# Two mixer layers and a mixture of experts: products in PSUM, an early weight split, solid first loads, stores ahead of a branch

## The chip, the cores and the metric

One core of one Trainium2 chip runs the kernel. The time is the device time of one execution in microseconds. The core has TensorE (PE, and PEld for its weight loads), VectorE (DVE), ScalarE (ACT), GpSimd (POOL) and SyncE (SP, which issues the loads here). SBUF is the working memory, PSUM holds TensorE's results in eight banks of 2 KB a partition.

## The reference

256 tokens of width 1024 go through two layers. Each layer projects the tokens, runs a gated causal convolution (31 taps on 512 channels) and a retention of 4 heads with rotary embedding, gates the retention, projects back and normalises. Layer 0 then has a dense SwiGLU, layer 1 a mixture of eight SwiGLU experts, two a token:

```python
for l in range(DEPTH):
    mix = hybrid_mixer(x, w_in[l], w_out[l], conv_w[l], conv_b[l], ...)
    x = layer_norm(ALPHA * x + mix, ln1_g[l], ln1_b[l])
    f = swiglu(x, ...) if l % 2 == 0 else moe_swiglu(x, router, moe_w1, moe_w3, moe_w2)
    x = layer_norm(ALPHA * x + f, ln2_g[l], ln2_b[l])
# in the mixer:   qh = rotary(q);  kh = rotary(k);  r = silu(g) * group_norm(retention(qh, kh, v))
# in the experts: gate = softmax(top-2 logits);  y = sum of gate * (silu(xe @ w1[e]) * (xe @ w3[e])) @ w2[e]
```

## The kernel before, in words

**Operands.** Every large product is three matmuls of rounded parts (`mm3`, L152): each float is split into a high part and a remainder. `parts` (L107) does it: ACT casts the high part, then DVE, or POOL where a unit says so, subtracts. All weights come as units of 1 MB ([128, 2048] floats), and each half of a unit is split by itself. So for every half that TensorE uses there is an ACT cast (L109) and a subtraction (L110).

**The order of weights.** It is written out by hand. `plan` appends halves to a stream, `W.take()` hands out the next one, and `W.ahead(n)` makes sure that n halves beyond the used ones are loaded and split; `emit` issues the load of a unit on SP when its first half is split. Every engine works through its instructions in program order. So where `W.ahead` stands decides where the casts and subtractions stand in ACT's, DVE's and POOL's queues. SP only waits for a buffer to come free and runs far ahead. Load buffers go round in a ring (`seq`, `pools`); behind the mixers the ring gets further places (`raw2`), in memory that the mixers leave.

**Start (L228 to L238).** The transposed tokens (`xf`) and the first two weight units arrive in quarters of 256 KB, alternating on SP. Each is split as it comes. 40 filler matmuls run ahead of the first product.

**Mixer (L367 to L640, once per layer).** The 124 multiply-adds of the convolution are DVE instructions (L391, one operand and the result in PSUM) that `fill` puts between the other steps in counted portions; the last taps of one channel group run on TensorE (`taps`, L403). `rotary` (L437) makes q and k of one token tile: a product into the scratch tile t2 in SBUF (L441), a product into qk (L444), and their sum (L446). The gate: TensorE projects g (`proj`), `taps` follows, then ACT writes silu(g) into the SBUF tile `sgt` (L584) and DVE multiplies `rz` by it (L585), per token tile, with a portion of `fill` behind each. TensorE transposes `rz` (`turn_r`, L497) and starts the output product (`wout_r`, L506). Meanwhile DVE ends the convolution, whose last sum is L394; its result is transposed (L516), normalised and joins the output product.

**Router (end of the mixer in layer 1).** The last normalisation (`ln_end`, L272 and L278) is done per token tile; the first tile's is followed by its transposes, logits (L320) and split for the gather, on POOL (L627). Then `W.ahead(2)` puts the split of the first expert unit there, `choose` (L303) picks the two experts on DVE, and the second tile does the same; `W.ahead(4)` splits the second unit. Filler matmuls, a prefix sum (L724 to L728), `rk` (L731), a permutation matrix P (L742) and gather matmuls (L751) follow.

**Experts.** 56 blocks of eight halves of w1 and w3 and four of w2. It ends with the sum of the last expert (`add`, L774; for tile 1 ACT and POOL), statistics, and `moments` (L971). Then comes a branch (L982) around a large body that is run only when an expert gets more than 128 tokens, which it does not here. Behind the branch stand the last normalisation (L1019, L1026) and the four stores: two on SP, two on ACT's queue.

Of the kernel before, what the change touches and what calls it, by code (L numbers as in the profile page):

```python
# [37 lines left out]
POOL_END = ((1, 0),)  # L38
ACT_END = (1,)
# [13 lines left out]
class Unit:  # L53
    def __init__(self, src, eng=None, n=1, at=None):
        self.src, self.eng, self.n, self.at, self.raw = src, eng, n, at, None
# [19 lines left out]
def tile_hybrid(ctx: ExitStack, tc, xT_in, x_in, ws, wm, cols, lnp, gnp, router, ident_in, rot, mask_in, out):  # L75
# [51 lines left out]
    def fetch(unit):  # L127
        if unit.raw is None:
            unit.raw = new_raw()
            n = 2048 // unit.n  # L130
            for q in range(unit.n):
                nc.sync.dma_start(unit.raw[:, n * q:n * q + n], unit.src[:, n * q:n * q + n])
        return unit.raw
# [88 lines left out]

    def part_w(i, q, r):
        o = W.made[2 * i + q // 2]
        parts(o[0][:, half(q % 2)], o[1][:, half(q % 2)], r[:, half(q)])

    for q in range(4):
        k = slice(2 * q, 2 * q + 2)  # L228
        nc.sync.dma_start(xf[:, k, :], xT_in[:, k, :])
        nc.sync.dma_start(r0[:, half(q)], ws[0][:, half(q)])  # L230
        parts(xh[:, k, :], xl[:, k, :], xf[:, k, :])
        part_w(0, q, r0)
    for q in range(4):
        nc.sync.dma_start(r1[:, half(q)], ws[1][:, half(q)])
# [132 lines left out]
    def mixer(l, psum, mp, me, heads, then):  # L367
# [209 lines left out]
        sgt = mp.tile([128, NT, 512], F32, tag="qkT", name="sgt")  # L577
# [16 lines left out]
        Wc += [W.take(0) for _ in range(4)]  # L594
        wout_r(0, 0)
# [30 lines left out]
        if l > 0:  # L626
            parts(xn[0][:, 0, :], xn[1][:, 0, :], x[:, 0, :], gp)  # L627
            W.ahead(2)
            choose(0, pl[:, 0, :])
        turn_x(NT - 1, psum)  # L630
# [3 lines left out]
        else:  # L634
# [3 lines left out]
            W.ahead(4)  # L638
# [94 lines left out]
    def gather(rk_of, n, pls, pt):  # L733
# [6 lines left out]
        for t in range(NT):  # L740
            for i in range(n):
                v.tensor_scalar(P[:, t, 128 * i:128 * i + 128], iota, rk_of(i, t), None, op0=ALU.is_equal)  # L742
# [3 lines left out]
        for k in range(0, KD, 2):  # L746
# [8 lines left out]
            for i in range(n):  # L755
                parts(gs[i][0][:, k:k + 2, :], gs[i][1][:, k:k + 2, :], p[:, :, i, :])
# [8 lines left out]
    def put(ys, PT, t):  # L765

        p = ptp.tile([128, 512], F32, tag="tp", name="pc")
# [4 lines left out]
    def add(p, t, h, g):  # L772
        o = acc[:, t, half(h)]
        v.scalar_tensor_tensor(o, p, g, o, op0=ALU.mult, op1=ALU.add)  # L774
# [74 lines left out]
    g0 = tokens_of(0)  # L849
    cnt = mo.tile([128, 1], F32, name="cnt")  # L850
# [105 lines left out]
    ps = [[put(ys[h], PT, t) for t in range(NT)] for h in range(2)]  # L956
    for h in range(2):
        for t in range(NT):
            o = acc[:, t, half(h)]
            if t in ACT_END:  # L960
                part = raw2[3 + h].tile([128, 512], F32, tag="raw", name="part")
                sc.mul(part, ps[h][t], gate_of(t))
                gp.tensor_tensor(o, o, part, op=ALU.add)
            else:
                add(ps[h][t], t, h, gate_of(t))
            v.bn_stats(sts[t][:, h, :], o)
# [4 lines left out]
    def moments():  # L971
        for t in range(NT):
            v.bn_aggr(mv[:, t, :], sts[t])
        v.tensor_scalar(ve, mv[:, :, 1], EPS, None, op0=ALU.add)
        gp.tensor_tensor(rs, ve, neghalf[:, :NT], op=ALU.pow)

    moments()


    if GENERAL:  # L980
        most = nc.values_load(cnti[0:1, 0:1], min_val=0, max_val=S)
        with tc.If(most > WIN):  # L982
            rk2 = mo.tile([128, NT, NE], F32, name="rk2")
            v.tensor_scalar(rk2, rk, -float(WIN), None, op0=ALU.add)
            with tc.For_i(0, NE, 1) as e:
                rc = mo.tile([128, NT, 2], F32, name="rc")
                for t in range(NT):
                    v.tensor_copy(rc[:, t, 0:1], rk2[:, t, ds(e, 1)])
                    v.tensor_copy(rc[:, t, 1:2], gate[:, t, ds(e, 1)])
                gg = gather(lambda i, t: rc[:, t, 0:1], 1, ((mo, "ga"),), mo)  # L990
# [3 lines left out]
                for b in range(NB):  # L994
# [3 lines left out]
                    def both(i):  # L998
                        s = Unit(src(i))
# [6 lines left out]
                    hT = split_h(turn(act(*ac)))  # L1006
# [3 lines left out]
                run(combine(yy, PT[:, 0, :], lambda t: rc[:, t, 1:2]))  # L1010
            for t in range(NT):
                for h in range(2):
                    v.bn_stats(sts[t][:, h, :], acc[:, t, half(h)])
            moments()

    for t in (1, 0):
        for h in range(2):
            o = acc[:, t, half(h)]
            v.scalar_tensor_tensor(o, o, mv[:, t, 0:1], gt[:, 0, half(h)], op0=ALU.subtract, op1=ALU.mult)  # L1019
    for t, h in ((1, 0), (1, 1), (0, 0), (0, 1)):  # L1020
        o = acc[:, t, half(h)]
        if (t, h) in POOL_END:
            sc.mul(o, o, rs[:, t:t + 1])
            gp.tensor_tensor(o, o, gt[:, 1, half(h)], op=ALU.add)
        else:
            v.scalar_tensor_tensor(o, o, rs[:, t:t + 1], gt[:, 1, half(h)], op0=ALU.mult, op1=ALU.add)  # L1026
        (nc.sync if t else nc.scalar).dma_start(out[tok(t), half(h)], o)
# [27 lines left out]
def _layout(inp):  # L1055
# [16 lines left out]
    ws = np.concatenate(units, 0)  # L1072
# [41 lines left out]
```

## Time and profile before

| | |
|---|---|
| Median of three executions | 1469.05 us (1467.22 to 1469.97) |
| Profiled execution | 1474.45 us, its span 1472.6 us |
| TensorE busy | 1436.3 us, 98% |
| VectorE busy | 1226.3 us, 83% |
| ScalarE busy | 973.6 us, 66% |
| GpSimd busy | 269.6 us, 18% |
| HBM read | 433.69 MB, 295 GB/s over the span |

The profile shows one execution. The span is from its first to its last instruction. In the windows each engine's busy time stands with its number of instructions in brackets; PEclk is the clock that TensorE was granted, as a share of 2.4 GHz (0.50 is 1.2 GHz); the DMA share is the mean busy share of 16 DMA engines. A row of the timeline has the start, the time from there to the end of the last of its xN instructions, the engine and line, and what is computed from what; in brackets the idle time in front and what ended it. A row of the waits says who waited for whom, the total, how often, and the longest.

### The profile page before, as it was taken

How to read it: one execution, taken by the hardware profiler on the slowest of the kernel's cores; microseconds unless marked ns; L12 is line 12 of the kernel's file. 1: busy time of each engine (PE TensorE's matmuls, PEld its weight loads, DVE VectorE, ACT ScalarE, POOL GpSimd, SP SyncE). 2: the span in 40 equal slices, each digit the busy share in tenths (PEclk: the TensorE clock that was granted, in tenths of full speed). 3: DMA queues.
4: the chain of work that ended last, by engine and by line, in shares of the span. 5: the costliest groups of instructions: out<-in, count | busy, mean ns of one | idle time of the engine just before them, and what ended most of it. 6: DMA issues, size and time to landing. Idle time of an engine off the chain costs nothing. (4 is left out here: it accounts for less than half of the span.)

```text
span 1472.6 us, 19730 instructions
## 1 busy us (share of the span) xinstructions
PE 1436.3 (98%) x7385; PEld 1211.4 (82%) x7385; DVE 1226.3 (83%) x1405; ACT 973.6 (66%) x1155; POOL 269.6 (18%) x136
## 2 busy tenths in 40 slices
PE   9999999999997999999999999999999999999995
PEld 8859999999866888888888888888888888888884
DVE  7976545547996799999999998999999899999996
ACT  6324444443524787877778777887887777778773
POOL 5630000001844111111111111111111111111111
PEclk9999999999997999999999999999999999999998
DMA  9535454454637879998999998999999899999951
GB/s 367 215 115 217 183 195 178 180 192 160 219 114 286 344 283 361 369 356 341 378 356 378 365 359 332 365 364 372 378 367 346 336 374 352 375 367 369 369 209 60
DMA packets 62311, 436.10 MB, mean 296 GB/s; under 512 B 7040, under 2 KB 7424, under 8 KB 9856
## 3 DMA queue, kind: packets, MB, share of 16 engines
q1 hardware_dynamic: 61920, 434.24, 77.5%
q8 instruction: 60, 0.98, 0.3%
q10 hardware_dynamic: 288, 0.52, 0.1%
q14 instruction: 43, 0.35, 0.1%
HBM read 433.69 MB, written 1.05 MB: 295 GB/s over the span
## 5 line engine op out<-in xcount | busy, mean ns | idle before, releaser
L110 DVE TENSOR_TENSOR wl<-raw,wh 128x1024 fp32r<-128x1024 f32 (+1 forms) x704 | 880.0, 1285 | 60.6 <-ACT wh L109 37.3
L109 ACT CAST wh<-raw 128x1024 fp32r<-128x1024 f32 (+1 forms) x802 | 822.0, 1046 | 155.1 <-PE ac L156 90.0
L110 POOL TENSOR_TENSOR wl<-raw,wh 128x1024 fp32r<-128x1024 f32 x98 | 242.3, 2488 | 1095.1 <-ACT wh L109 1019.4
L154 PE MATMUL ac<-wh,gah 128*128 128x512 f32 x448 | 177.4, 396 | 0.0
L155 PE MATMUL ac<-wl,gah 128*128 128x512 f32 x448 | 174.9, 390 | 0.5 <-POOL wl L110 0.5
L156 PE MATMUL ac<-wh,gal 128*128 128x512 f32 x448 | 175.0, 391 | 0.0
L156 PE MATMUL y<-wh,htl 128*128 128x512 f32 x448 | 174.4, 389 | 0.0
L155 PE MATMUL y<-wl,hth 128*128 128x512 f32 x440 | 171.7, 390 | 0.1
L154 PE MATMUL y<-wh,hth 128*128 128x512 f32 x440 | 171.4, 389 | 0.0
L154 PE MATMUL wk<-xh,wh 128*128 128x256 f32 x512 | 145.6, 284 | 0.7 <-ACT wh L109 0.7
L156 PE MATMUL wk<-xh,wl 128*128 128x256 f32 x512 | 145.1, 283 | 0.0
L155 PE MATMUL wk<-xl,wh 128*128 128x256 f32 x512 | 144.9, 283 | 0.0
L391 DVE SCALAR_TENSOR_TENSOR wk<-u,colt,wk 128x256 f32<-128x256 f32 x209 | 99.8, 488 | 5.7
L156 PEld LDWEIGHTS wk<-xh,wl 128*128 128x128 f32 x512 | 99.2, 194 | 0.5 <-DVE wl L110 0.5
L154 PEld LDWEIGHTS wk<-xh,wh 128*128 128x128 f32 x512 | 97.5, 190 | 2.4 <-ACT wh L109 1.3
L155 PEld LDWEIGHTS ac<-wl,gah 128*128 128x128 f32 x448 | 84.4, 188 | 17.7 <-POOL wl L110 0.9
L156 PEld LDWEIGHTS ac<-wh,gal 128*128 128x128 f32 x448 | 84.2, 188 | 17.9
L155 PEld LDWEIGHTS wk<-xl,wh 128*128 128x128 f32 x512 | 97.6, 191 | 0.9
L156 PEld LDWEIGHTS y<-wh,htl 128*128 128x128 f32 x448 | 84.1, 188 | 17.4
L154 PEld LDWEIGHTS ac<-wh,gah 128*128 128x128 f32 x448 | 84.5, 189 | 16.6
L155 PEld LDWEIGHTS y<-wl,hth 128*128 128x128 f32 x440 | 82.6, 188 | 18.8 <-DVE wl L110 1.9
L154 PEld LDWEIGHTS y<-wh,hth 128*128 128x128 f32 x440 | 82.6, 188 | 17.1
(202 smaller groups left out, 2049.6 us busy)
## 6 DMA issues: line engine op xcount, KB each, us to landing
raw<-in_wm_dram SPq DMA_DIRECT2D x336, 1024.0 KB, 6.6
raw<-in_ws_dram SPq DMA_DIRECT2D x68, 1024.0 KB, 4.9
raw<-in_lnp_dram SPq DMA_DIRECT2D x4, 1024.0 KB, 4.6
raw<-in_ws_dram SPq DMA_DIRECT2D x8, 256.0 KB, 5.7
xf<-in_xT_dram SPq DMA_DIRECT2D x4, 256.0 KB, 4.9
x<-in_x_dram SPq DMA_DIRECT2D x1, 1024.0 KB, 7.4
mask<-in_mask_dram SPq DMA_DIRECT2D x1, 768.0 KB, 12.1
gn<-in_gnp_dram SPq DMA_DIRECT2D x2, 256.0 KB, 8.3
```

Of the source, the lines that this page charges most:

```text
L109: sc.copy(hi, src)
L110: (eng or v).tensor_tensor(lo, src, f32(hi), op=ALU.subtract)
L154: pe.matmul(o, a[0], b[0], start=first, stop=False, skip_group_check=True)
L155: pe.matmul(o, a[0], b[1], start=False, stop=False, skip_group_check=True)
L156: pe.matmul(o, a[1], b[0], start=False, stop=last, skip_group_check=True)
L391: v.scalar_tensor_tensor(d, u[:, cc, k:k + S], w[:, k:k + 1], o, op0=ALU.mult, op1=ALU.add)
```

## The change

- Rotary's scratch tile t2 is a PSUM bank. Silu of the gate is written over its own PSUM bank, and DVE reads it there.
- In layer 1 `W.ahead(2)` moves from behind the normalisation to a place in front of the output product, and `W.ahead(4)` from the end of the mixer to behind the permutation matrix. Both halves of the first expert unit are subtracted on POOL, those of the second on DVE. The first token tile is split on DVE, behind its `choose`.
- The transposed tokens and the first two weight units lie in memory so that each quarter is one solid block of 256 KB.
- At the end token tile 0 is summed in PSUM, tile 1 by ACT and POOL; statistics and moments go tile by tile; the normalisation and the four stores, all on SP, come ahead of the branch. The branch's body is moved from DVE to POOL and ACT, with its loads on ACT's queue, and it normalises and stores the result once more if it runs.

```diff
-            plan(Unit(wm[e, 6 * b + q], tuple(gp if first and q == 0 or MOEP.get(q) == h else None for h in range(2)),
+            plan(Unit(wm[e, 6 * b + q], tuple(gp if (q == 0 if first else MOEP.get(q) == h) else None for h in range(2)),
                       at=0 if first and q else None))
...
+    def quarter(i, q):
+
+        return ws[i].rearrange("p f -> (p f)")[128 * 512 * q:128 * 512 * (q + 1)].rearrange("(p f) -> p f", p=128)
...
-        nc.sync.dma_start(xf[:, k, :], xT_in[:, k, :])
-        nc.sync.dma_start(r0[:, half(q)], ws[0][:, half(q)])
+        nc.sync.dma_start(xf[:, k, :], xT_in[q])
+        nc.sync.dma_start(r0[:, half(q)], quarter(0, q))
...
-        nc.sync.dma_start(r1[:, half(q)], ws[1][:, half(q)])
+        nc.sync.dma_start(r1[:, half(q)], quarter(1, q))
...
-            t2 = me.tile([128, 8, 2, 32], F32, tag="t2", name="t2")
+            t2 = bank(psum, [128, 8, 2, 32])
...
-        sgt = mp.tile([128, NT, 512], F32, tag="qkT", name="sgt")
...
-            sc.activation(sgt[:, t, :], pg[t], AF.Silu)
-            v.tensor_tensor(rz[:, t, :], rz[:, t, :], sgt[:, t, :], op=ALU.mult)
+            sc.activation(pg[t], pg[t], AF.Silu)
+            v.tensor_tensor(rz[:, t, :], rz[:, t, :], pg[t], op=ALU.mult)
...
         Wc += [W.take(0) for _ in range(4)]
+        if l > 0:
+            W.ahead(2)
         wout_r(0, 0)
...
         if l > 0:
-            parts(xn[0][:, 0, :], xn[1][:, 0, :], x[:, 0, :], gp)
-            W.ahead(2)
             choose(0, pl[:, 0, :])
+            parts(xn[0][:, 0, :], xn[1][:, 0, :], x[:, 0, :])
...
             choose(1, pl[:, 1, :])
-            W.ahead(4)
...
     g0 = tokens_of(0)
+    W.ahead(4)
...
+    ps = [[put(ys[h], PT, t, (None, new_ac)[h]) for t in range(NT)] for h in range(2)]
...
+    def moments(t):
+        v.bn_aggr(mv[:, t, :], sts[t])
+        v.tensor_scalar(ve[:, t:t + 1], mv[:, t, 1:2], EPS, None, op0=ALU.add)
+        gp.tensor_tensor(rs[:, t:t + 1], ve[:, t:t + 1], neghalf[:, :1], op=ALU.pow)
+
+    def send(t, h, o):
+        nc.sync.dma_start(out[tok(t), half(h)], o)
+
+    def norm1(t, h, to, o):
+        v.scalar_tensor_tensor(to, o, mv[:, t, 0:1], gt[:, 0, half(h)], op0=ALU.subtract, op1=ALU.mult)
+
+    def norm2(t, h, to, o):
+        v.scalar_tensor_tensor(to, o, rs[:, t:t + 1], gt[:, 1, half(h)], op0=ALU.mult, op1=ALU.add)
...
+    for h in range(2):
+        add_slow(ps[h][1], 1, h, gate_of(1), raw2[3 + h].tile([128, 512], F32, tag="raw", name="part"))
+    for t in range(NT):
+        for h in range(2):
+            if t == 0:
+                add(ps[h][0], 0, h, gate_of(0), ps[h][0])
+            stats(t, h, ps[h][0] if t == 0 else None)
+        moments(t)
...
+    norm1(1, 0, n0, acc[:, 1, half(0)])
+    v.scalar_tensor_tensor(nm, mv[:, 1, 0:1], -1.0, rs[:, 1:2], op0=ALU.mult, op1=ALU.mult)
+    o = fin[:, 1, half(1)]
+    sc.activation(o, acc[:, 1, half(1)], AF.Identity, scale=rs[:, 1:2], bias=nm[:, 0:1])
+    gp.tensor_tensor(o, o, gt[:, 0, half(1)], op=ALU.mult)
+    gp.tensor_tensor(o, o, gt[:, 1, half(1)], op=ALU.add)
+    n = new_y()
+    for h in range(2):
+        norm1(0, h, n[h], ps[h][0])
+        norm2(0, h, fin[:, 0, half(h)], n[h])
+        send(0, h, fin[:, 0, half(h)])
+    norm2(1, 0, fin[:, 1, half(0)], n0)
+    for h in range(2):
+        send(1, h, fin[:, 1, half(h)])
+
+    for h in range(2):
+        sc.copy(acc[:, 0, half(h)], ps[h][0])
...
-    for t, h in ((1, 0), (1, 1), (0, 0), (0, 1)):
-        o = acc[:, t, half(h)]
-        if (t, h) in POOL_END:
-            sc.mul(o, o, rs[:, t:t + 1])
-            gp.tensor_tensor(o, o, gt[:, 1, half(h)], op=ALU.add)
-        else:
-            v.scalar_tensor_tensor(o, o, rs[:, t:t + 1], gt[:, 1, half(h)], op0=ALU.mult, op1=ALU.add)
-        (nc.sync if t else nc.scalar).dma_start(out[tok(t), half(h)], o)
...
+    for i in range(2):
+        ws[i] = ws[i].reshape(128, 4, 512).transpose(1, 0, 2).reshape(128, 2048)
...
-        "xT": c(x.T.reshape(KD, 128, S).transpose(1, 0, 2)),
+        "xT": c(x.T.reshape(4, 2, 128, S).transpose(0, 2, 1, 3)),
```

## Rows read from the trace of the kernel before

**Rows 1.** The windows, expert loop: stretch, length, five busy engines, PEclk, DMA, GB/s

```profile
500.00:1400.00 900.00, 898.94 (x4101) 742.65 (x4100) 826.69 (x763) 710.68 (x774) 128.11 (x52) 1.00 0.94 359
```

**Rows 2.** The waits of TensorE, whole span: waiter, releaser, us, times, longest

```profile
PE wk L497 <- DVE rz L585: 6.6, 4, 2.1
PE wk L291 <- DVE x L278: 5.0, 2, 4.6
PE wk L320 <- DVE rl L314: 1.4, 1, 1.4
```

**Rows 3.** The waits of the drain, 1452 to 1473 us

```profile
DVE acc L1019 <- DVEq L982: 3.6, 1, 3.6
```

**Rows 4.** The timeline of DVE, gate products of layers 0 and 1: start, us

```profile
75.84 3.56 DVE L585 TENSOR_TENSOR rz<-rz,sgt 128x512 f32<-128x512 f32 x2 [1.18 <-ACT sgt L584]
421.38 2.80 DVE L585 TENSOR_TENSOR rz<-rz,sgt 128x512 f32<-128x512 f32 x1
...
424.50 2.44 DVE L585 TENSOR_TENSOR rz<-rz,sgt 128x512 f32<-128x512 f32 x1
```

**Rows 5.** The timeline of POOL beside the gate of layer 1 and the router

```profile
418.96 7.43 POOL L110 TENSOR_TENSOR wl<-raw,wh 128x1024 fp32r<-128x1024 f32 x3
...
462.54 5.54 POOL L110 TENSOR_TENSOR wl<-raw,wh 128x1024 fp32r<-128x1024 f32 x2
```

**Rows 6.** The timeline of DVE, rotary of layer 0

```profile
36.70 0.68 DVE L444 TENSOR_TENSOR qk<-wk,rott 128x512 f32<-128x512 f32 x1
37.42 2.84 DVE L446 TENSOR_TENSOR qk<-qk,t 128x512 f32<-128x512 f32 x1
```

**Rows 7.** The timeline of TensorE, conv taps of layers 0 and 1

```profile
70.55 5.35 PE L407 MATMUL wk<-u,dg 128*128 128x256 f32 x24
...
417.75 4.92 PE L407 MATMUL wk<-u,dg 128*128 128x256 f32 x22
```

**Rows 8.** The timeline of TensorE, output products of both layers

```profile
80.36 12.86 PE L506 MATMUL wk<-raw,mr 128*128 128x512 f32 x24
...
427.90 11.47 PE L506 MATMUL wk<-raw,mr 128*128 128x512 f32 x24
```

**Rows 9.** The windows, TensorE alone: stretch, length, PE busy, PEclk, DMA, GB/s

```profile
85.00:86.00 1.00, 1.00 (x3) 0.91 0.49 74
...
429.00:430.00 1.00, 1.00 (x2) 0.54 0.97 410
```

**Rows 10.** The timeline of DVE, last conv sum of layer 1

```profile
437.92 0.42 DVE L394 TENSOR_TENSOR cv<-cv,wk 128x256 f32<-128x256 f32 x1
```

**Rows 11.** The timeline of DVE, last normalisation of layer 1 and the router

```profile
460.28 2.84 DVE L272 SCALAR_TENSOR_TENSOR s<-s,mv,raw 128x512 f32<-128x512 f32 x1
463.16 2.71 DVE L278 SCALAR_TENSOR_TENSOR x<-s,rs,raw 128x512 f32<-128x512 f32 x1
...
474.17 1.22 DVE L110 TENSOR_TENSOR wl<-raw,wh 128x1024 fp32r<-128x1024 f32 x1
```

**Rows 12.** The timeline of DVE, first sum of the tail

```profile
1454.89 0.74 DVE L774 SCALAR_TENSOR_TENSOR acc<-pc,gate,acc 128x512 f32<-128x512 f32 x1
```

**Rows 13.** The timeline of TensorE, logits of tile 1 and first gather

```profile
468.45 3.55 PE L320 MATMUL wk<-rt,xf 128*128 128x8 f32 x16 [1.41 <-DVE rl L314]
...
476.13 0.55 PE L751 MATMUL pg<-P,xh 128*128 128x256 f32 x1 [0.49 <-DVE P L742]
```

**Rows 14.** The windows with TensorE alone, in front of the gather

```profile
475.00:476.00 1.00, 0.64 (x7) 0.50 1.02 434
```

**Rows 15.** The waits of the first 40 us

```profile
PE wk L154 <- ACT wh L109: 0.7, 2, 0.5
```

**Rows 16.** The windows with TensorE alone, first loads

```profile
9.00:10.00 1.00, 1.00 (x5) 1.00 1.01 379
```

**Rows 17.** The timeline of ACT's DMA queue, last stores

```profile
1468.58 1.00 ACTq L1027 DMA_DIRECT2D out_dram<-acc  x2
```

**Rows 18.** The waits of SP's DMA queue, expert loop

```profile
SPq L132 <- DVE wl L110: 785.9, 313, 9.6
```

More of the change, by code (lines that the diff above doesn't have):

```diff
@@ L131, in fetch @@
             for q in range(unit.n):
-                nc.sync.dma_start(unit.raw[:, n * q:n * q + n], unit.src[:, n * q:n * q + n])
+                (unit.queue or nc.sync).dma_start(unit.raw[:, n * q:n * q + n], unit.src[:, n * q:n * q + n])
         return unit.raw
@@ L763, in gather, with put @@
         sc.copy(PT, p)
-    def put(ys, PT, t):
-        p = ptp.tile([128, 512], F32, tag="tp", name="pc")
+    def put(ys, PT, t, new=None):
+        p = new() if new else ptp.tile([128, 512], F32, tag="tp", name="pc")
         for i in range(2):
@@ L969, in tile_hybrid, with add_slow, stats @@
     ve = sm.tile([128, NT], F32, tag="vel", name="vel")
[L971 to L977, printed above, removed]
+    def add_slow(p, t, h, g, part):
+        o = acc[:, t, half(h)]
+        sc.mul(part, p, g)
+        gp.tensor_tensor(o, o, part, op=ALU.add)
+    def stats(t, h, src=None):
+        v.bn_stats(sts[t][:, h, :], acc[:, t, half(h)] if src is None else src)
@@ new lines, in tile_hybrid @@
+    for h in range(2):
[6 more added lines that the diff above has]
+        moments(t)
+    fin = raw2[5].tile([128, NT, D], F32, tag="raw", name="fin")
+    nm = sm.tile([128, 1], F32, tag="nm", name="nm")
+    n0 = new_ac()
+    norm1(1, 0, n0, acc[:, 1, half(0)])
@@ L980, in tile_hybrid, with flat @@
+    for h in range(2):
+        send(1, h, fin[:, 1, half(h)])
+    for h in range(2):
+        sc.copy(acc[:, 0, half(h)], ps[h][0])
     if GENERAL:
+        def flat(p, shape):
+            o = raw2[5].tile(shape, F32, tag="raw", name="flat")
+            sc.copy(o, p)
+            return o
         most = nc.values_load(cnti[0:1, 0:1], min_val=0, max_val=S)
@@ L998, in both @@
                     def both(i):
-                        s = Unit(src(i))
+                        s = Unit(src(i), gp, queue=nc.scalar)
                         return [emit("first", s), emit("second", s)]
@@ L1005, in tile_hybrid @@
                             up(ac[i // 2], 2 * (i % 2) + j, w, gs[0])
-                    hT = split_h(turn(act(*ac)))
+                    hh = mo2.tile([128, 512], F32, tag="hh", name="hh")
+                    sc.activation(hh, ac[0], AF.Silu)
+                    gp.tensor_tensor(hh, flat(ac[1], [128, 512]), hh, op=ALU.mult)
+                    hT = split([128, 4, 128], flat(turn(hh), [128, 4, 128]), mo2, "ht", eng=gp)
                     for i in range(2):
@@ L1009, in tile_hybrid @@
                             down(hT, 2 * i + j, w, yy, b == 0, b == NB - 1)
-                run(combine(yy, PT[:, 0, :], lambda t: rc[:, t, 1:2]))
+                for h in range(2):
+                    yh = split([128, 512], flat(yy[h], [128, 512]), late[0], f"ys{h}", eng=gp)
+                    for t in range(NT):
+                        add_slow(put(yh, PT[:, 0, :], t), t, h, rc[:, t, 1:2],
+                                 raw2[3 + h].tile([128, 512], F32, tag="raw", name="part"))
             for t in range(NT):
                 for h in range(2):
[L1013 to L1019, printed above, removed]
-    for t, h in ((1, 0), (1, 1), (0, 0), (0, 1)):
-        o = acc[:, t, half(h)]
-        if (t, h) in POOL_END:
-            sc.mul(o, o, rs[:, t:t + 1])
-            gp.tensor_tensor(o, o, gt[:, 1, half(h)], op=ALU.add)
-        else:
-            v.scalar_tensor_tensor(o, o, rs[:, t:t + 1], gt[:, 1, half(h)], op0=ALU.mult, op1=ALU.add)
-        (nc.sync if t else nc.scalar).dma_start(out[tok(t), half(h)], o)
+                    stats(t, h)
+                moments(t)
+            for t in range(NT):
+                for h in range(2):
+                    o = acc[:, t, half(h)]
+                    norm1(t, h, o, o)
+                    norm2(t, h, o, o)
+                    send(t, h, o)
 def _consts():
```

34 lines of the change are left out of this document (12 added, 22 removed).

## The prediction

> **What bounds the kernel now.** I read the windows first. In the expert loop TensorE is busy 898.94 of 900 us, and the change leaves that loop's work alone [rows 1]. So the loop passes on what happens in front of it, and time can be won only where TensorE stands still: before the loop and after it. TensorE's waits say where: 6.6 us on the gate products (L585), 5.0 us on the last normalisation of layer 1 (L278), 1.4 us on the router (L314) [rows 2]. The rest is the drain: DVE alone waits 3.6 us at the surplus branch before it normalises [rows 3].
>
> Why do L585 and L278 take so long? DVE's rows at L585 are 3.56 us for two, then 2.80 and 2.44 us [rows 4], while POOL runs its subtractions without a gap [rows 5]. In the rotary stage, again beside POOL, the product that reads one operand from PSUM takes 0.68 us, and right behind it the sum of the same size with both operands in SBUF takes 2.84 [rows 6]. So an SBUF pair waits for POOL, and a PSUM operand avoids it.
>
> **The gate, layer 1.** Silu now stays in the PSUM bank, so each product has one SBUF operand and I take 0.7 us. The first starts at 421.38 and ends at 422.1; a conv tap of 0.5 and the second follow, done by 423.3 instead of 426.9 [rows 4]. TensorE's taps end at 417.75 + 4.92 = 422.67 [rows 7], so the eight transposes follow at once (two lots of 0.6), with ACT's copy of the first under the second, and the output product starts at about 423.95 instead of 427.90 [rows 8]: 3.95 us. It also ran at a granted clock of 0.50 (the 1.2 GHz level) after that idling until 429.9 [rows 9]: 2.0 us at half speed lose 1.0. With no idling in front I expect the 2.4 GHz level throughout. Together 4.9 us on TensorE. DVE must follow: its last conv sum ends at 437.92 + 0.42 = 438.34 [rows 10], 0.9 before TensorE's transposes at 439.21. It wins 2.80 + 2.44 - 1.4 = 3.84 here and about 0.4 from rotary (more is lost at L421, where it would wait for ACT), so it ends at 434.1 against TensorE's 434.3. A tie: I take 4.9, with 3.9 the lower end (clock not regained) and 5.0 the upper.
>
> **The gate and rotary, layer 0.** DVE is behind TensorE there, so rotary's 2.84 and 1.1 becoming 0.7 each [rows 6] (2.6 us) moves everything up to L585 forward. Then the products wait for silu only and end before TensorE's taps do, at 70.55 + 5.35 = 75.90 [rows 7]. The transposes take 1.2, the output product starts at 77.15 instead of 80.36 [rows 8]: 3.2 us. Its clock was 0.50 until about 85.1 [rows 9]: 4.75 us at half speed, 2.4 lost. Sum 5.6; I take 5.5, bounds 3.2 and 5.6. DVE's conv behind it needs 12.2 us from the products' end, so it too is done before the output product. Each rotary call takes one more of the eight banks; with two for conv and two for the projection in use, four are free, so I cost that at nothing if banks are handed out in turn (a rival below).
>
> **The router.** W.ahead(2) moves in front of the output product. Both casts go to an ACT that idles there, both subtractions (2.4 us each) to POOL beside conv taps, which read one SBUF operand; POOL is through 2.9 us before it is needed for conv's normalisation. Their load is long in SBUF. The split of the normalised first tile goes from POOL to DVE, behind choose(0). So POOL no longer collides with the second half of the normalisation: L272 and L278 took 2.84 and 2.71 [rows 11] beside POOL's subtractions, the last two 5.54 us [rows 5]; at 0.74 each, like the tail's undisturbed sum [rows 12], that is 4.1 us less. Transposes start at 461.8 instead of 465.9. DVE then runs choose(0) (2.2 us, its slowest instruction losing 1.4 us of waiting), the two splits (1.2 each) and is free for choose(1) at 466.4; the logits, 3.55 us at the low clock [rows 13], end about then. So sel is there at 468.75, where it was at 474.25. There a weight split of 1.22 stood in front of rk until 475.30 [rows 11]; W.ahead(4) now comes after the permutation, which takes that off. rk starts at 469.15, and the gather, first held by P and then by the ten filler matmuls, at 470.2 instead of 476.13 [rows 13]. **5.9 us.** The two weight splits now stand in front of the first gathered subtraction: 2.45 us where 3.2 us from P to that subtraction were idle or short work, so 0.3 late, under TensorE's first gather. Without that cover it would cost those 0.3. The load of the second unit is still issued where its buffer comes free; only its place in the ring moves by one. The clock is 0.50 through this stretch [rows 14] and I leave it so. Bounds: 4.9 if the new DVE order holds TensorE once, 8.0 if the half-speed stretch behind the gather ends early.
>
> **The start.** The quarters become solid blocks. TensorE waited 0.7 us for the first two quarters [rows 15], and I reckon 0.5 more in smaller gaps before it ran unbroken. No row has a solid block in 2 KB pieces, so the price is unknown: nothing, or a loss of 0.5 if the other order of addresses suits less; at best 1.2 (all gaps), plus 1.3 if the slow matmuls of the start end earlier. The rate rises to 379 GB/s by 9 us with the old pieces still coming [rows 16], so most of the slow start is not their layout. I take 0.6.
> The Trainium skill, DMA: Bandwidth & Descriptors, section "Why a DMA increments its semaphore by 16 and not by 1", says one descriptor moves one contiguous run of the last dimension; a partition of SBUF still takes 2 KB, so by it nothing changes and the sum is 0.6 smaller. No run here shows which.
>
> **The tail.** The normalisation no longer stands behind the branch. Token tile 0 is summed in PSUM, tile 1 by ACT and POOL, and PSUM banks of the accumulators take away TensorE's wait of 0.8. Counted from DVE's first sum at 1454.9 with 0.7 to 0.75 us per 128x512 instruction [rows 12]: two sums and two statistics to 1457.9, moments to 1458.3, two statistics and moments of tile 1 to 1460.2, one product to 1460.9, POOL's power to 1461.3, then five products to 1465.2. The fourth quarter (ACT 0.7, POOL 2.5) is done by 1464.9. SP's last issue, 0.4 long, ends at about 1466.1; before, the last of two ended at 1469.58 [rows 17]. 3.5 us; bounds 2.3 (jump, below) and 4.3 (no wait on POOL's power).
>
> **Sum.** 0.6 + 5.5 + 4.9 + 5.9 + 3.5 = 20.4 us. The profiled execution took 1474.45 us (span 1472.6 and 1.85 around it), so 1454.0 like it; the median of the runs is 5.4 lower, 1469.05, and becomes **1448.6**. Lower ends: -0.5 + 3.2 + 3.9 + 4.9 + 2.3 = 13.8; upper: 2.5 + 5.6 + 5.0 + 8.0 + 4.3 = 25.4. That gives 1443.6 to 1455.3.
>
> **Rivals.**
> *The clock falls anyway.* The short transposes are thin work. Then 1.0 and 2.4 stay lost: 1452.0. For: the low clock outlasts the idling in both layers [rows 9]; against: it fell only after TensorE had stood still.
> *The jump ends last.* DVE's wait at the branch is not for data [rows 3]: its sequencer branches at 1460.3 and goes on 3 us later. Now the jump lies behind the sends, and ACT and POOL carry more of the skipped body. If SP pays 3.6 us after its last issue, the end comes 0.8 later than that, at about 1470.2, and 2.4 of the tail are won: 1449.8. Against: SP's body has shrunk.
> The Trainium skill, Runtime: NRT & Kernel Launch, section "Instruction fetch mechanics", has the rule: a taken branch to a target not held yet must fetch it. The 3.6 us of the row agree.
> *Banks.* If the bank freed last is given out first, the V projection waits for rotary's second tile, about 8.2 us in layer 0 and 3.6 in layer 1, with 3 us of clock: 14.8 given back, 1463.4. Against: TensorE today starts that projection long before rotary is done.
> *Loads.* If the loop were fed too late, only the tail would count: 1465.5. For: DMA is 94% busy [rows 1]. Against: the queue waits 785.9 us for DVE to free buffers [rows 18], so it runs ahead.
> *Not the port.* If PSUM products stay slow, the gate and rotary terms (10.4) vanish: 1459.0.
> *Slower: one engine.* A solid block can be lowered as one long run. If its pieces then went to one of the 16 DMA engines, a sixteenth of 379 GB/s [rows 16] is 24, and the twelve quarters (3.1 MB) take 131 us where 8 would do: 1449 + 123 = 1572. It decides below five engines (33 us for four, 25 more than now, over the 20 won). Against: the pattern keeps 128 rows as its outer dimension.
>
> **How the numbers follow.** Forecast 0.58, clock 0.14, jump 0.10, banks 0.05, loads 0.05, not the port 0.04, one engine 0.03, and 0.01 that several losses meet within 0.2% (2.9 us, about what a measurement can tell). All but the last two are faster: 0.96, 0.01, 0.03. The first three hold 0.82 and lie inside the bounds, so the range is 1443.5 to 1455.5.
>
> **What would show it.** Right: no TensorE wait on L585's successor, the product at 0.7; granted clock 1.00 after both output products start; L272 and L278 at 0.75; gather about 17 us earlier than now; no DVE wait before the normalisation. Wrong: a new TensorE wait on rotary, on DVE's split of the second unit, or on loads in the loop; a first quarter landing later; engines waiting at a branch behind the last send.

## The result, and the profile after

| | before | after |
|---|---|---|
| median of the timed runs, us | 1468.13 (1467.16 to 1469.97, 4 runs) | 1453.37 (1452.91 to 1453.59, 4 runs) |
| profiled execution / its span, us | 1474.45 / 1472.6 | 1453.59 / 1451.8 |

The ratio is 0.9898, 95% interval [0.988, 0.9915]: the medians move by 14.8 us, the two profiled executions by 20.9 us. The forecast was 1448.6 us, with a range of 1443.5 to 1455.5. So the sum of 20.4 us fits the two profiled executions and misses the medians by almost 6 us; the experiments are about that gap.

The waits of TensorE after, where the change bears on them (waiter, releaser, us in total, times, longest):

```profile
PE wk L153 <- POOL wl L108: 1.9, 1, 1.9
...
PE wk L293 <- DVE x L280: 1.0, 2, 0.6
...
PE pg L752 <- DVE cnt L854: 0.9, 1, 0.9
```

The gate's 6.6 us and the normalisation's 5.0 [rows 2] became nothing and 1.0. Two waits are new: 1.9 us on POOL's first weight split, and 0.9 us behind the gather.

The timeline of after, in the order of time (start, us, engine, line):

```profile
12.70 0.38 ACT L422 ACTIVATE sgl<-wk 128x256 f32<-128x256 f32 x1
...
18.00 2.36 POOL L108 TENSOR_TENSOR wl<-raw,wh 128x1024 fp32r<-128x1024 f32 x1 [16.16 <-ACT wh L107]
...
69.94 5.34 PE L409 MATMUL wk<-u,dg 128*128 128x256 f32 x24
...
71.10 1.28 DVE L586 TENSOR_TENSOR rz<-rz,wk 128x512 f32<-128x512 f32 x2 [1.17 <-ACT wk L585]
...
75.13 1.04 PE L499 MATMUL wk<-ident,rz 128*128 128x128 f32 x8
76.40 10.57 PE L508 MATMUL wk<-raw,mr 128*128 128x512 f32 x24 [0.24 <-ACT mr L500]
...
411.48 4.92 PE L409 MATMUL wk<-u,dg 128*128 128x256 f32 x22
...
414.72 0.68 DVE L586 TENSOR_TENSOR rz<-rz,wk 128x512 f32<-128x512 f32 x1
...
415.71 0.68 DVE L586 TENSOR_TENSOR rz<-rz,wk 128x512 f32<-128x512 f32 x1
...
416.23 1.04 PE L499 MATMUL wk<-ident,rz 128*128 128x128 f32 x8
417.51 10.57 PE L508 MATMUL wk<-raw,mr 128*128 128x512 f32 x24 [0.24 <-ACT mr L500]
427.91 1.04 PE L518 MATMUL wk<-ident,cv 128*128 128x128 f32 x8
...
449.00 0.74 DVE L274 SCALAR_TENSOR_TENSOR s<-s,mv,raw 128x512 f32<-128x512 f32 x1
449.78 0.75 DVE L280 SCALAR_TENSOR_TENSOR x<-s,rs,raw 128x512 f32<-128x512 f32 x1
...
458.92 0.58 PE L752 MATMUL pg<-P,xh 128*128 128x256 f32 x1
...
461.30 0.39 PE L752 MATMUL pg<-P,xh 128*128 128x256 f32 x1 [0.85 <-DVE cnt L854]
...
1436.93 0.75 DVE L776 SCALAR_TENSOR_TENSOR pc<-pc,gate,acc 128x512 f32<-128x512 f32 x1
...
1444.60 3.25 SPq L978 DMA_DIRECT2D out_dram<-fin  x4
```

Read against the rows of before: each gate product takes 0.64 to 0.68 us, not 1.8 to 2.8 [rows 4]; the eight transposes follow the taps in one go; the output products take 10.57 us, not 12.86 and 11.47 [rows 8]; L274 and L280 take 0.74 and 0.75 where they took 2.84 and 2.71 [rows 11]; the gather starts at 458.92, not 476.13 [rows 13]; DVE's first sum comes at 1436.93, not 1454.89 [rows 12], and the stores are issued with no wait at the branch [rows 3].

The windows of after (stretch, length, busy time of PE, PEld, DVE, ACT and POOL, granted clock, DMA share, GB/s):

```profile
84.00:85.00 1.00, 1.00 (x3) 0.38 (x2) 0.48 (x2) 0.00 (x0) 0.00 (x0) 1.00 0.48 197
...
416.00:430.00 14.00, 13.76 (x45) 7.00 (x44) 12.05 (x27) 3.91 (x5) 10.25 (x5) 1.00 0.11 35
...
455.00:459.00 4.00, 3.80 (x38) 3.47 (x37) 3.04 (x16) 0.16 (x1) 0.00 (x0) 0.50 1.01 420
...
500.00:1400.00 900.00, 899.43 (x4106) 743.42 (x4105) 828.09 (x757) 708.93 (x771) 128.14 (x52) 1.00 0.95 360
```

The granted clock is 1.00 beside both output products, where it was at the 1.2 GHz level before [rows 9], still 0.50 in front of the gather [rows 14], and the loop is as full as it was [rows 1].

From trace to trace the 20.8 us of span come apart so. Taps of layer 0: 70.55 to 69.94, the start won 0.6. Taps of layer 1: 417.75 to 411.48, another 5.65, layer 0. The gather comes 17.2 us earlier in all: from those taps to it, it was 58.4 us and is 47.4. Of these 10.9 the gate of layer 1 has 5.0 (TensorE turns to the conv sums 21.5 us behind the taps' start before, 16.4 after) and the router the 5.9 that are left. To DVE's first sum it is 17.95, 0.75 more. From there to the end of the span it is 17.71 before and 14.87 after: 2.8 for the tail.

### The profile page after: what moved, and what is told of

It reads as the page before. It is cut to its first block, busy times and chain, and to the rows that moved or that the text cites. A ratio compares the mean times of both kernels' runs of the same rounds, so it can differ in the third digit from the quotient of the medians.

```text
span 1451.8 us, 19734 instructions
## 1 busy us (share of the span) xinstructions
PE 1427.4 (98%) x7385; PEld 1205.5 (83%) x7385; DVE 1211.7 (83%) x1408; ACT 974.7 (67%) x1157; POOL 261.8 (18%) x136
## 2 busy tenths in 40 slices
DMA packets 62312, 436.10 MB, mean 300 GB/s; under 512 B 7041, under 2 KB 7425, under 8 KB 9857
## 5 line engine op out<-in xcount | busy, mean ns | idle before, releaser
L108 DVE TENSOR_TENSOR wl<-raw,wh 128x1024 fp32r<-128x1024 f32 (+1 forms) x705 | 881.1, 1285 | 59.8 <-ACT wh L107 36.1
L108 POOL TENSOR_TENSOR wl<-raw,wh 128x1024 fp32r<-128x1024 f32 x97 | 235.0, 2440 | 1096.9 <-ACT wh L107 1005.6
L154 PE MATMUL ac<-wh,gal 128*128 128x512 f32 x448 | 174.8, 390 | 0.0
L154 PE MATMUL y<-wh,htl 128*128 128x512 f32 x448 | 174.4, 389 | 0.0
L154 PE MATMUL wk<-xh,wl 128*128 128x256 f32 x512 | 143.8, 281 | 0.2 <-DVE wl L108 0.2
L154 PEld LDWEIGHTS ac<-wh,gal 128*128 128x128 f32 x448 | 84.1, 188 | 17.9
L154 PEld LDWEIGHTS y<-wh,htl 128*128 128x128 f32 x448 | 84.1, 188 | 17.4
L154 PEld LDWEIGHTS wk<-xh,wl 128*128 128x128 f32 x512 | 98.0, 191 | 0.4 <-DVE wl L108 0.4
```

Source lines behind the costliest of these rows:

```text
L108: (eng or v).tensor_tensor(lo, src, f32(hi), op=ALU.subtract)
L154: pe.matmul(o, a[1], b[0], start=False, stop=last, skip_group_check=True)
```

## The experiments

Times are medians with their range; the ratio and its 95% interval are to runs of before on the same chip, and the ratio is not quite the quotient of the medians. Those of before were 1469.67 (for experiments 1 to 4), 1469.4 (5 to 8) and 1470.2 us (9 to 12). Its 81 runs spread from 1466.7 to 1482.1 us; the four of after lie within 0.7 us.

**1. The kernel before once more** (no edit).

> The kernel before, unchanged, to see its profile once more. The sum of the prediction (20.4 us) fits the two profiled executions (1474.45 to 1453.59 us, 20.9), but the medians moved by 14.8 only. Theory A: the profiled execution of before had lost 5 to 6 us by chance that its timed runs did not lose; then this profile is nearer to 1468 us (span about 1466), and one of the stretches of low clock (78 to 85 us, 427 to 430, 461 to 481) or the slow products of the start (to 13.3 us) is shorter or gone in it. Theory B: being profiled costs this kernel 5 to 6 us each time; then the span is again 1472 to 1473 us and all four stretches look as they did.

Measured: 1469.43 us (1467.13 to 1474.82), ratio 0.999 [0.9972, 1.0009]. The profiled execution was again a long one, 1474.82 us, so theory A's "nearer to 1468" failed this time; but theory B's identical stretches failed too. This execution started better (first sigmoid at 14.08 us, not 15.87) and was later all the same at the taps of layer 0 (72.79); from there to the taps of layer 1 it lost about as much (346.60 us, the profiled before 347.20). Its first rotary sum of layer 0, by the groups of that line (number, ns min/median/max):

```profile
L446 DVE TENSOR_TENSOR qk<-qk,t x4: 694/1972/7251, 35.6 to 386.2; 128x512 f32<-128x512 f32 x4
```

and by the timeline, with POOL's row in which it ended:

```profile
35.63 7.25 DVE L446 TENSOR_TENSOR qk<-qk,t 128x512 f32<-128x512 f32 x1
...
42.28 2.82 POOL L110 TENSOR_TENSOR wl<-raw,wh 128x1024 fp32r<-128x1024 f32 x1
```

The same instruction took 2.84 us in the profile the prediction was made from [rows 6] and 7.25 here. It ended 0.6 us after POOL had gone from one subtraction to the next (42.28), and that one took 2.82 us instead of 2.4. This made a new theory: the sum waits until it is let in between two of POOL's subtractions, which of them is chance (a draw), and before's scatter is this draw.

**2. The solid quarters alone.** Edit, on before:

```
-        nc.sync.dma_start(xf[:, k, :], xT_in[:, k, :])
-        nc.sync.dma_start(r0[:, half(q)], ws[0][:, half(q)])
+        nc.sync.dma_start(xf[:, k, :], xT_in[q])
+        nc.sync.dma_start(r0[:, half(q)], quarter(0, q))
...
-        nc.sync.dma_start(r1[:, half(q)], ws[1][:, half(q)])
+        nc.sync.dma_start(r1[:, half(q)], quarter(1, q))
```

> Before plus the solid quarters alone. My forecast's term: 0.6 us faster, 1467.5 us. Rival 1 (by the Trainium skill's rule of one descriptor for each run of the last dimension): no change, within 0.2 us. Rival 2: the 3.2 us by which the first sigmoid came earlier are all kept when the rest of the start is as before: 1465 us. In the profile: first sigmoid at 12.7 us (15.9 before), then a wait of TensorE of about 1.9 us on POOL's first split, and the taps of layer 0 about 0.6 us earlier than 70.55.

Measured: 1468.05 us (1466.37 to 1478.0), ratio 0.9992 [0.9973, 1.0011]: inconclusive, it fits 0.6 us and none. First sigmoid at 12.96 us, then the wait of 1.9 us on POOL's split, taps at 70.39. The profile, at 1466.73 us, shows more than it was made for. Its timeline:

```profile
34.50 1.08 DVE L450 TENSOR_TENSOR qk<-qk,t 128x512 f32<-128x512 f32 x1
...
35.00 2.87 POOL L110 TENSOR_TENSOR wl<-raw,wh 128x1024 fp32r<-128x1024 f32 x1
...
70.39 5.34 PE L411 MATMUL wk<-u,dg 128*128 128x256 f32 x24
...
71.56 3.60 DVE L589 TENSOR_TENSOR rz<-rz,sgt 128x512 f32<-128x512 f32 x2 [1.19 <-ACT sgt L588]
...
75.57 1.04 PE L501 MATMUL wk<-ident,rz 128*128 128x128 f32 x8
...
411.95 4.92 PE L411 MATMUL wk<-u,dg 128*128 128x256 f32 x22
```

The old rotary sum, this time let in at once (1.08 us, ending 0.58 after POOL's boundary at 35.00). DVE is then early enough that the old, slow gate products (3.60 for two) are done before the taps, TensorE does not wait, its clock stays. From the taps of layer 0 to those of layer 1 it is 341.56 us, where after takes 341.54 and the profiled before 347.20. With a lucky draw the old layer 0 loses nothing at all. In layer 1 the gate still waits, and its first rotary sum still takes 2.84 us, as in every profile with the old rotary (2.84 to 2.86): only layer 0's sum is a draw.

**3. Gate and rotary in PSUM alone.** Edit, on before:

```
-            t2 = me.tile([128, 8, 2, 32], F32, tag="t2", name="t2")
+            t2 = bank(psum, [128, 8, 2, 32])
...
-            sc.activation(sgt[:, t, :], pg[t], AF.Silu)
-            v.tensor_tensor(rz[:, t, :], rz[:, t, :], sgt[:, t, :], op=ALU.mult)
+            sc.activation(pg[t], pg[t], AF.Silu)
+            v.tensor_tensor(rz[:, t, :], rz[:, t, :], pg[t], op=ALU.mult)
```

> Before plus silu left in the PSUM bank and rotary's t2 in PSUM, nothing else. Forecast's terms 5.5 + 4.9 = 10.4 us: 1457.7 us, granted clock 1.00 behind both output products, products at L585 of 0.7 us. Rival (the timed runs of before do not lose the 3.4 us of low clock that its profiled execution lost): 7.0 us, 1461.1 us. Rival (some of it is given back before the loop, since router and first splits stay as they were): under 7 us, with a later gather than the 10.4 us earlier that the forecast gives.

Measured: 1461.87 us (1461.31 to 1462.89), ratio 0.9938 [0.9918, 0.9958]: by the medians 7.8 us, not 10.4 (the interval, 6.2 to 12.1 us, holds both), and the spread falls from over 15 us to 1.6. The profile does all that the forecast said: products at 0.68, clock 1.00, gather at 465.36, 10.8 earlier than in the profiled before. Nothing is given back before the loop; it is the before of the medians that had less to lose. The first rival came nearest, with 1461.1 us. Its reason, the low clock, is a part of what experiment 2 shows: in a lucky execution layer 0 loses neither the 2.4 us of low clock nor the 3.2 us of waiting. The granted clocks of the runs point the same way: a mean of 0.986 in the profiled before, 0.988 in the median of the 35 timed runs, 0.990 here.

**4. The router alone.** Edit, on before:

```
+        if l > 0:
+            W.ahead(2)
         wout_r(0, 0)
...
-            parts(xn[0][:, 0, :], xn[1][:, 0, :], x[:, 0, :], gp)
-            W.ahead(2)
             choose(0, pl[:, 0, :])
+            parts(xn[0][:, 0, :], xn[1][:, 0, :], x[:, 0, :])
...
-            W.ahead(4)
...
     g0 = tokens_of(0)
+    W.ahead(4)
```

and the first unit's second half is planned for POOL as well.

> Before plus the early split of the first expert unit and the other order of splits in the router, nothing else. Forecast's term: 5.9 us, 1462.2 us, gather at 470.2 instead of 476.1 in a profile whose layer 1 is like that of before. Rival (the two POOL splits now stand beside the slow gate products of layer 1, which are still in SBUF, and slow them): 2 to 4 us, 1464 to 1466. A wait of TensorE of about 0.9 us behind the first gather, on DVE's two weight splits, is expected by both.

Measured: 1464.26 us (1463.04 to 1475.66), ratio 0.9979 [0.9953, 1.0004], a median 5.4 lower, still with three outliers at 1475; the interval also holds no change. From the taps of layer 1 (414.22) to the gather (466.74) it is 52.5 us, before 58.4: 5.9, the forecast's term. POOL's early splits did not slow the gate further (2.79 and 2.44 us).

**5. Rotary alone.** Edit, on before:

```
-            t2 = me.tile([128, 8, 2, 32], F32, tag="t2", name="t2")
+            t2 = bank(psum, [128, 8, 2, 32])
```

> Before plus rotary's t2 in a PSUM bank, nothing else. In four profiles of kernels with the old rotary, the first sum of layer 0 (128x512, both operands in SBUF) took 2.84, 7.25 and 1.08 us beside POOL's subtractions, and before itself spreads from 1466.7 to 1482 us. Theory A (the draw at that one sum decides how far DVE lags behind in layer 0, and so whether TensorE waits for the gate there and loses its clock): the sum is 0.7 us every time, the spread of the timed runs falls to under 2 us, no wait of TensorE on L585 in layer 0, no low clock at 78 to 86 us, and the median is that of a lucky run of before: 1465.5 to 1467.0 us; the slow gate products stay. Theory B (the gate's products in SBUF lose layer 0's time, rotary little): a median within 1.5 us of before's, 1468 to 1470, and still a spread of 5 us or more.

Measured: 1467.96 us (1465.74 to 1469.33), ratio 0.9975 [0.9953, 0.9997]. The long outliers go (before had five runs from 1479.6 to 1481.5 beside it), the sum is 0.69 us. But theory A asked for more than came: the spread is 3.6 us, the median 1 us above its range, and TensorE still waits 0.8 us on the gate in layer 0, by the timeline:

```profile
74.86 0.60 PE L497 MATMUL wk<-ident,rz 128*128 128x128 f32 x4
76.26 0.66 PE L497 MATMUL wk<-ident,rz 128*128 128x128 f32 x4 [0.80 <-DVE rz L585]
```

The outliers go with rotary: with t2 in PSUM none of 61 runs (after and experiments 3, 5, 7 and 9 to 12) lies more than 1.4 us above its median; with t2 in SBUF 19 of 140 lie more than 8 us above. With the gate in PSUM as well (experiment 3) the spread is 1.6 us, so the rest of the scatter goes with the gate. How is not shown: its two products of layer 0 take 3.55 to 3.60 us in every profile with the old gate.

**6. After with rotary's t2 back in SBUF.** Edit, on after:

```
-            t2 = bank(psum, [128, 8, 2, 32])
+            t2 = me.tile([128, 8, 2, 32], F32, tag="t2", name="t2")
```

> After with rotary's t2 back in SBUF, everything else as in after. Theory A (the draw): the spread comes back, single runs 2 to 10 us above the fastest, and the median is 0 to 3 us above after's 1453.4; its fastest run is within 1 us of after's. Theory B (rotary little): 1453.4 to 1454.5 us and a spread of under 2 us, like after.

Measured: 1454.35 us (1452.01 to 1465.17), ratio 0.9898 [0.9866, 0.993]. Eight of twelve runs lie from 1452.0 to 1455.0 us, four from 1464.1 to 1465.2: the scatter is back, the fastest is as fast as after. Theory A. In its profile, of a run of 1452.0 us, that sum took 2.24 us.

**7. After without the surplus branch.** Edit, on after:

```
-    if GENERAL:
+    if False:
```

> After with the surplus branch left out (more than 128 tokens for one expert would not be computed, and the count is not read). Behind the last send after took 3.95 us to the end, before 3.0. Rival of the prediction (the jump ends last): without it the end comes 0.9 us or more earlier, 1452.4 us or less. Theory (the last send lands 3.3 us after its issue where before's took 2.0 to 2.1, four stores following each other on one queue): no change, 1453.0 to 1453.6 us, and the last landing again 3.0 to 3.3 us.

Measured: 1465.12 us (1464.29 to 1466.47), ratio 0.996 [0.9936, 0.9984], 11.7 us slower than after: neither theory. The tail answers all the same: from DVE's first sum to the end 13.38 us, after 14.87. The stores land 2.0 to 2.3 us after their issue. DMA queues and issues of the last 7 and 8 us (packets, MB, share; KB each, median us to landing), first without the branch, then after:

```profile
q1 hardware_dynamic: 576, 1.05, 40.0%
...
out_dram<-fin SPq DMA_DIRECT2D x4, 256.0 KB, 2.0
```

```profile
q1 hardware_dynamic: 576, 1.05, 36.0%
q14 instruction: 6, 0.05, 1.9%
...
out_dram<-fin SPq DMA_DIRECT2D x4, 256.0 KB, 2.8
```

With the branch, six packets of instructions come in among the stores, and these take up to 3.3 us. So the branch costs 1.5 us at the end, 1.2 of it behind the last issue: not by an engine arriving last, as the rival said, but by landings that take longer. That the six packets are what delays them is argued from their being there; how 0.05 MB can do so is not shown. What made the kernel slower as a whole is in the loop: 986.5 us from the first product with expert weights to the last permutation, after 973.2, with no new wait. TensorE's windows, 1000 to 1100 us, without the branch and after:

```profile
1000.00:1100.00 100.00, 100.00 (x449) 81.83 (x448) 90.27 (x79) 79.20 (x85) 14.45 (x6) 1.00 0.94 369
```

```profile
1000.00:1100.00 100.00, 100.00 (x454) 82.76 (x453) 92.21 (x81) 79.45 (x85) 13.26 (x6) 1.00 0.98 370
```

One per cent fewer products in the same time, at the same clock, without idling; from 500 to 1400 us it is 4051 against 4106. Leaving the branch out also leaves out its tiles and its code, so that what remains can lie elsewhere in memory; whether one of these slows the products was not tried and stays open.

**8. The tail alone.** The change's hunks from the sum of the last expert on, on before.

> Before plus the new tail alone (stores ahead of the surplus branch, sums of tile 0 in PSUM). Forecast's term: 3.5 us. From the two traces 2.8 us (first DVE sum to the end of the span 17.71 before, 14.87 after). In the profile I expect 14.7 to 15.0 us from DVE's first sum to the end. The median carries before's scatter, so 1465 to 1468 us fits both.

Measured: 1467.27 us (1465.91 to 1479.98), ratio 0.9984 [0.9958, 1.0011]: undecided by the time. In the profile, from DVE's first sum to the end, it is 14.93 us, as in after. The profile caught the longest run, and its timeline shows what an outlier is made of:

```profile
33.03 16.48 POOL L108 TENSOR_TENSOR wl<-raw,wh 128x1024 fp32r<-128x1024 f32 x7
...
36.37 13.68 DVE L444 TENSOR_TENSOR qk<-qk,t 128x512 f32<-128x512 f32 x1
```

One sum of 128x512 stood for 13.68 us beside POOL's unbroken row, and ended 0.54 us after that row did (33.03 + 16.48 = 49.51). TensorE idled 8 us for it; the taps of layer 0 start at 80.97.

**9. The weight splits behind the first gather blocks.** Edit, on after:

```
     g0 = tokens_of(0)
-    W.ahead(4)
```

> After without its early split of the second expert unit (the call in front of the count): the splits then come with the first weights taken in the loop, behind the first two gathered blocks. In after, the count stood behind those two splits on DVE (2.35 us) and TensorE waited 0.85 us for it, before the second gather block. Theory: that wait goes, the first product with expert weights comes 3.4 us after the gather's start minus 0.5 to 0.9 us, and the time is 1452.5 to 1452.9 us. Rival (the splits are then late for the third piece of weights): a wait of TensorE on DVE's weight split of 0.5 us or more a few us later, and no change.

Measured: 1453.55 us (1452.6 to 1454.55), ratio 0.9878 [0.9854, 0.9902]. From gather to the first product 2.71 us instead of 3.43, as the theory said; from there to the last permutation 975.1 instead of 973.2. A new wait, `PE ac L154 <- DVE gal L108` of 0.7 us, is part of that; where the rest goes is open. No gain: the rival's outcome, by another wait of DVE.

**10. POOL's first unit loaded in two halves.** Edit, on after:

```
-                plan(Unit(ws[b + q], gp if q >= POOL_GLU else None, 2 if l == 0 and q == 1 else 1))
+                plan(Unit(ws[b + q], gp if q >= POOL_GLU else None, 2 if l == 0 and q in (1, 4) else 1))
```

> After with the first unit that POOL splits loaded in two pieces instead of one. In after TensorE waited 1.9 us at 18.5 us for POOL's first subtraction, whose cast had waited for that load. Theory: the first half lands earlier by half of a 2.5 us transfer, the wait falls to 0.7 us, and 1.2 us are kept to the end: 1452.2 us. Rival (DVE or POOL is behind in layer 0 and takes it back): the wait falls, but the output product of layer 0 starts no earlier than 76.4 us, 1453.4 us.

Measured: 1451.72 us (1451.27 to 1452.88), ratio 0.9869 [0.9845, 0.9892]. The lowest median, 1.7 us below after's; the intervals of the two ratios overlap, so the gain is likely and not settled. In part it is a draw again: in experiments 6, 7 and 9, with after's start, the wait on POOL's split was 0.6 to 0.8 us, not 1.9. POOL starts 2.3 us earlier than in after, the wait is gone, and the taps come at 67.28, where the five profiles with after's start have 68.40 to 70.19, by the timeline:

```profile
15.68 16.72 POOL L108 TENSOR_TENSOR wl<-raw,wh 128x1024 fp32r<-128x1024 f32 x7 [13.84 <-ACT wh L107]
...
67.28 5.35 PE L409 MATMUL wk<-u,dg 128*128 128x256 f32 x24
72.46 1.04 PE L499 MATMUL wk<-ident,rz 128*128 128x128 f32 x8
```

**11. Stores on two queues.** Edit, on after (with ACT's copies for the branch moved in front):

```
-        nc.sync.dma_start(out[tok(t), half(h)], o)
+        (nc.sync if t else nc.scalar).dma_start(out[tok(t), half(h)], o)
```

> After with the two stores of tile 0 on ACT's queue and ACT's copies for the surplus branch in front of them. Without the branch the four stores landed 2.0 to 2.3 us after their issue, with it 2.0 to 3.3. Theory (the jumps of the engines fetch instructions through the same DMA engines and delay the last store): landing of the last store again about 3 us, only SP's backlog of 0.3 to 0.4 us is won: 1453.0 us. Rival (four stores on one queue are what delays it): landing 2.0 to 2.2 us, 1452.4 us.

Measured: 1454.39 us (1453.93 to 1455.69), ratio 0.9885 [0.9861, 0.9908], 1.0 slower. Its profile's tail is 16.75 us, 1.9 longer than after's, and 1.4 of this is the edit's own doing: DVE now waits for a copy of ACT (`DVE y L981 <- ACT acc L1007: 1.4`). The landings answer the question, by the DMA issues:

```profile
out_dram<-fin ACTq DMA_DIRECT2D x2, 256.0 KB, 2.5
out_dram<-fin SPq DMA_DIRECT2D x2, 256.0 KB, 3.5
```

A second queue does not shorten them; the rival fell, and the instructions' packets (again six) remain as the explanation.

**12. The three together.** The edits of 9, 10 and 11, on after.

> After with the three edits together (weights split behind the gather, first unit in halves, stores on two queues). If the three add up: 0.5 to 0.9, 1.2 and 0.3 to 1.0, so 1450.3 to 1451.4 us. If the start's gain is taken back: 1451.5 to 1452.6 us.

Measured: 1455.52 us (1454.69 to 1456.56), ratio 0.9893 [0.9869, 0.9917]: both sums missed. The start's gain is there (taps at 67.58), the loop takes 975.1 us as in 9, and the tail 17.23 us: the losses of 9 and 11 add up too.

## Why the prediction came out as it did

**The direction and the range held; the point was 4.8 us low**, and one step of it is the cause: "the median of the runs is 5.4 lower, 1469.05, and becomes 1448.6". It took the sum made against one profiled execution off the median, as if what set that execution apart from the timed runs lay outside the sum. It lay in a term: layer 0's 5.5 us. The profiled before had lost 5.65 us there; experiment 2's execution, with the same gate and rotary, lost nothing, and took 1466.73 us. So much of the loss was counted twice, once as 5.5 to be won and once as 5.4 already absent from the median. Against the execution that it was made from, the forecast was right: 1454.0 us "like it", and the profiled after took 1453.59. By medians gate and rotary are worth 7.8 us (experiment 3); less layer 1's 5.0 this leaves, as an estimate, some 2.8 for layer 0, half the term. Its bounds, 3.2 and 5.6, came from one execution too; the lower one should have been 0. With 2.8 there and the tail's 2.8 (below) the same sum is 17.0 us, and 1452.1. The 1.3 us from there to 1453.4 are not pinned down; part of them may lie behind the gather (see the router). That the range held owes something to its width of 12 us.

**Gate, layer 1: 4.9**, measured 5.0. The products, the transposes at once, the clock: each as forecast. DVE's tie with TensorE came out level: its conv sums end at 427.80 (by the timeline) where TensorE turns to them at 427.91.

**Router: 5.9**, measured 5.9 in the trace of after and 5.9 in experiment 4. The 0.3 us lateness that the two weight splits were priced at was 0.85: not the first gathered subtraction but the count behind them held TensorE, since the second block needs the bank that the count reads. Here too the profiled before was a slow execution. From the first gather to the first product with expert weights it took 3.56 us, at a granted clock of 0.50; experiments 1, 2, 3 and 5, with the same router, took 2.08 to 2.12 at 1.00, and the new router, with its wait on the count, takes 3.4 in after and in experiments 4, 6, 7, 10 and 11. From layer 1's taps to that product the old gate and router took 61.9 us in the profiled before and 60.4 to 61.5 in experiments 1, 2 and 5, after 50.9: the two terms of 10.8 together are worth 11.1 against the one and 9.5 to 10.6 against the others.

**Start: 0.6**, net 0.6 in this pair of profiles, as 3.2 won and 2.6 given back; neither is typical, so the right number is luck. The first sigmoid comes at 12.7 instead of 15.87, most of it because the profiled before ran 22 of its first products 0.21 us apart, until 13.3 us, and after two. They are 0.12 apart elsewhere; the profile gives 1.00 as the granted clock of that stretch, so the cause of the slow pace is open. Nor does it go with the layout alone: experiment 1, with the old quarters, ran seven so, and experiment 11, with the new ones, 17. The first sigmoid lies between 14.1 and 15.9 us in the six profiles with the old quarters, between 12.6 and 15.1 in the eight with the new. TensorE then runs into POOL's first split, which the load does not let start sooner (experiment 10 removes that). The step "I reckon 0.5 more in smaller gaps" is not what happened.

What the layout does change is the rate. In the first two windows of 5 us after moved 174 and 366 GB/s, before 147 and 316; over all profiles it is 165 to 202 and 346 to 372 with solid quarters, 147 to 160 and 288 to 316 without. The median landing of a quarter of the tokens fell from 4.9 to 4.1 us. The Trainium skill, DMA: Bandwidth & Descriptors, section "Why a DMA increments its semaphore by 16 and not by 1", has one descriptor for each run of the last dimension. With that the trace agrees: the executions moved 62311 packets before and 62312 after. What the prediction drew from it, that nothing changes, does not hold for the rate; in the time the difference is too small to show (0.9992 [0.9973, 1.0011]).

**Tail: 3.5**, measured 2.8. To the end of the last issue 11.2 us were forecast from DVE's first sum, and 10.9 measured; the landing was taken as before's 2.0 us and was 3.3. The loss lies within the bound of 2.3 that was set for the jump.

**The rivals.** The clock did not fall (1.00 beside both output products). The jump did not end last, yet the branch costs 1.5 us through the stores, by the tail of experiment 7. The Trainium skill, Runtime: NRT & Kernel Launch, section "Instruction fetch mechanics", says that a taken jump may have to fetch its target by DMA; the six packets of the instruction queue, which experiment 7 does not have among its stores, agree. Banks: no wait on a bank at rotary. Loads: the loop is as full as before. Not the port: products of 0.68. One engine: the first loads run faster, not slower. "Several losses" did not meet.

**That the PSUM operand avoids POOL** was inferred from one pair of rows [rows 6]. After's rows bear it out: four sums of 0.689 us, beside the same POOL rows. The group of that line in after, and in experiments 2 and 8 (ns min/median/max):

```profile
L448 DVE TENSOR_TENSOR qk<-qk,wk x4: 689/689/689, 34.4 to 376.6; 128x512 f32<-128x512 f32 x4
```

```profile
L450 DVE TENSOR_TENSOR qk<-qk,t x4: 692/1112/2841, 34.5 to 379.0; 128x512 f32<-128x512 f32 x4
```

```profile
L444 DVE TENSOR_TENSOR qk<-qk,t x4: 691/1774/13682, 36.4 to 393.0; 128x512 f32<-128x512 f32 x4
```

## What to carry to other kernels

Before a stall seen in one profile is priced, take a second profile of the same kernel. Within one profile a large maximum beside a small minimum only says that something collides: L446 took 0.69 to 2.85 us, L272 0.74 to 2.84. In the other profiles with the old router this L272 came out the same each time (2.84 or 2.85) and is a price; layer 0's L446 did not and is a draw. The term of a draw has zero as one end, and an offset between the profiled execution and the median may be that same draw: a sum made against one must not be taken off the other. A DVE instruction with two SBUF operands does not belong beside an unbroken row of POOL work; here one operand in PSUM made its time fixed. And stores moved ahead of a branch can still land later because of it.

## What the runs showed that was not expected

The wait of DVE for POOL is not over with POOL's current instruction. POOL's subtractions take 2.4 us each; the first rotary sum of layer 0 took 1.08, 2.00, 2.24, 2.84, 7.25 and 13.68 us in six profiles. Those of 1.08, 7.25 and 13.68 us ended 0.54 to 0.60 us after a boundary of POOL's row or its end, so the longer ones were passed over at several boundaries. The Trainium skill, SBUF — State Buffer, section "Who interferes with whom", has the exclusive port that two SBUF inputs need; that the loser can miss several turns is what these rows add.

With six packets of instructions (0.05 MB) among them, 256 KB stores landed in 2.0 to 3.3 us, without them in 2.0 to 2.3. And leaving out code and tiles that are never used in this execution made TensorE's products 1% slower at the same clock, for a reason that stays open.
